# First stage of a two-layer diffusion backbone: the middle tokens' norm and scaling ordered ahead of the last tokens' squares, and the last tokens' norm issued inside the first projection

## Chip, cores, metric

The kernel runs on one core of a Trainium2 chip. The metric is the device time of one execution in microseconds (us), lower is better. The engines named below are TensorE (PE, matmuls into PSUM banks; PEld is its weight load), VectorE (DVE), ScalarE (ACT), GpSimd (POOL) and SyncE (SP, whose queue issues most of the DMAs). Each runs its own queue in order and waits for others through semaphores.

## What is computed

Two layers over 1024 latent tokens and 256 context tokens of width 1024. Cut to what matters for the change, the even layer begins with:

```python
def rms_norm(x, g):
    y = x * lax.rsqrt(jnp.mean(x * x, axis=-1, keepdims=True) + EPS)
    return y * g

sh, sc, g = jnp.split(silu(cond) @ mod_w + mod_b, 3, axis=-1)   # modulation; cond is c or c_ctx
h = rms_norm(x, norm_g) * (1.0 + sc) + sh                       # for latent and for context tokens
aq, ak, av, ag, bq, bk, bv, bg = split_cols(h @ w_in, EVEN_WIDTHS)   # queries, keys, values, gates
```

Behind it come two attentions (global, and banded with a sink), their gates, the output projection, the odd layer (a convolution module and neighbourhood attention) and a last norm.

## The kernel before

Activations are held transposed: 128 partitions by tokens, in DK = 8 row blocks `dk` of the width. The 1280 tokens are cut into three chunks (`CHUNKS`): chunk 0 is the context (256 tokens), chunk 1 the "middle" tokens (512), chunk 2 the "last" tokens (512). Every fp32 product is made as three matmuls: an operand is split into a rounded hi part and the rest, the lo part, and `mm3` runs hi by hi, hi by lo, and lo by hi (L334 to L336).

The first stage is a list of steps, `PLAN = 'p0mmnbwmm1h2nbhnbh'`, worked off in order (loop `for ev in PLAN`, L741). Digits load a chunk of x, `w` loads the first projection weights, and the others are:

- `m`: half a block of the modulation (`mod_half`): 8 matmuls `pm` with an output of 32 partitions (L184; 16 records in the profile), a copy `mrow` on ACT, 4 small matmuls `trm` (L189), and adds into `modT` and `gs`.
- `n`: `norm_x`: for each of 8 row blocks a square on ACT (L727 for the first, into `acc`, L730 for the others, into `sq`), and 7 dependent adds `acc += sq` on DVE (L731). `sq` has three buffers.
- `b`: `norm_bc`, which runs `rstd_steps`: matmuls `trs` (L261) sum `acc` over the partitions; DVE makes mean plus EPS in `rbv` (L264); `newton_rsqrt` takes a power on POOL (L246) and three small DVE steps (L247 to L249); matmuls `bc` (L271) spread the result over 128 partitions.
- `h`: `make_h`: for each row block a scaling on DVE (L324), a shift on ACT (L327, or L330 and a rounding in `split`, L314) that gives the hi part, and the lo part on DVE (L328) or POOL (L317), by the letters of `HV = 'gggvvvvg'`. The hi and lo parts are `hc` for chunk 0, `hh` and `hl` for the others.

The first projection follows: `fill0(0, w0)` runs `proj_qkv` and `proj_gate` for head group `ORDER[0]`. `proj_qkv` takes ten blocks `j` of 128 tokens (j = 0, 1 context, 2 to 5 middle, 6 to 9 last), each 8 x 3 matmuls `pq` of 384 columns with weights `wh`, `wl`; behind each pair come copies `pc` on ACT, V, the rotary steps, and later a transpose `trk` (L881) in `qk_tail`. `proj_gate` makes `pg`. Between the row blocks `tick()` advances `mods`, which loads and multiplies the rest of the modulation (again `pm`, `trm`).

The code gives each instruction its dependences and a priority; a scheduler places it in its engine's queue by its own estimate of when it can run, so code order and queue order differ. What is written under `tc.issue_after(ins)` is scheduled no earlier than `ins`. After the first projection, attention steps are woven with the other head groups' projections (`weave`), and the second layer follows.

Of the kernel before, what the change touches and what calls it, by code (L numbers as in the profile page):

```python
# [10 lines left out]
F32 = mybir.dt.float32  # L11
F32R = mybir.dt.float32r
ALU = mybir.AluOpType
# [59 lines left out]
TICK0, TICK1 = (1, 3)  # L73
PLAN = 'p0mmnbwmm1h2nbhnbh'
MWR = "ABxAVx"
XA = 4
ORDER = (2, 3, 0, 1)
QORD = (2, 3, 4, 0, 5, 6, 1, 7, 8, 9)
# [10 lines left out]
def tile_kernel(ctx: ExitStack, tc: tile.TileContext, a, out):  # L89
# [161 lines left out]

    last = []

    def rstd_steps(pool, accs, n, tag, inv=1.0, tr="tr"):


        nb = n // P
        tr = bank(tr, nm("trs"))
        for b in range(nb):
            for k, acc in enumerate(accs):  # L260
                last.append(PE.matmul(tr[:, 2 * b : 2 * b + 2], acc[:, b * P : (b + 1) * P], ones, start=(k == 0),  # L261
                                      stop=(k == len(accs) - 1)))
        v = pool.tile([P, 8], F32, tag="rbv", name=nm("rbv"), bufs=2)
        VE.tensor_scalar(v[:, :nb], tr[:, 0 : 2 * nb].rearrange("p (b two) -> p b two", two=2)[:, :, 0],  # L264
                         inv, EPS, op0=ALU.mult, op1=ALU.add)
        r = newton_rsqrt(pool, v[:, :nb], nb, "rb")
        yield
        yield
        bc = bank(tag, nm("bc"))
        for b in range(nb):  # L270
            PE.matmul(bc[:, b * P : (b + 1) * P], r[:, b : b + 1].broadcast_to([P, P]), ident, start=True, stop=True)  # L271
        return bc
# [45 lines left out]

    def make_h(l, c, xs, bc, h):

        cond = 1 if c == 0 else 0
        for dk in range(DK):
            x = xs(dk)
            VE.scalar_tensor_tensor(x, x, gs[l][:, dk, cond : cond + 1], bc, op0=ALU.mult, op1=ALU.mult)  # L324
            shift = modT[l][:, dk, cond : cond + 1]
            if HV[dk] == "v":
                SC.activation(h[0][:, dk, :], x, AF.Identity, bias=shift)  # L327
                VE.scalar_tensor_tensor(h[1][:, dk, :], x, shift, h[0][:, dk, :].bitcast(F32), op0=ALU.add, op1=ALU.subtract)  # L328
# [366 lines left out]
    with ExitStack() as p0x:  # L695
# [6 lines left out]
        with tc.tile_pool(name="st0", bufs=1, reuse_waits="tile") as st0:  # L702
# [19 lines left out]
            def norm_x(c):  # L722
                n = CHUNKS[c][1]
                acc = kvp.tile([P, 512], F32, tag="QH", name=nm("acc"), bufs=3)
                for dk in range(DK):
                    if dk == 0:
                        SC.activation(acc[:, :n], xraw[c][0], AF.Square)  # L727
                    else:
                        sq = kvp.tile([P, 512], F32, tag="QL", name=nm("sq"), bufs=3)
                        SC.activation(sq[:, :n], xraw[c][dk], AF.Square)  # L730
                        VE.tensor_tensor(acc[:, :n], acc[:, :n], sq[:, :n], op=ALU.add)  # L731
                return acc
# [5 lines left out]
            made = [0]  # L738
            accs, bcs, mh = [], [], [(0, 0), (0, 1), (1, 0), (1, 1)]
            mwp[0] = st0  # L740
            for ev in PLAN:  # L741
# [90 lines left out]
        def proj_qkv(u, w):  # L832
            wh, wl = w or load_w0("ev_qkv", u)
            new_kv(u)
            for jp in range(5):
                pc = ap.tile([P, 2, 384], F32, tag="pc", name=nm("pc"), bufs=PCB)
                for jj in range(2):
                    j = 2 * jp + jj
                    pp = bank("pp", nm("pq"))
                    for dk in range(DK):  # L840
                        mm3(pp[:, :384], Hs(h, 0, j * P, P, dk), Hs(h, 1, j * P, P, dk), wh[dk], wl[dk],
                            dk == 0, dk == DK - 1)
                        if dk % 3 == 1:
# [56 lines left out]

        for _ in fill0(0, w0):
            pass
        solo[0] = False
# [725 lines left out]
```

## Time and profile before

| | us |
|---|---|
| median of 3 runs (1553.38 to 1559.51) | 1554.67 |
| the profiled execution's own time | 1557.54 |
| its span in the profile | 1555.8 |
| TensorE busy in the span | 1462.5 |
| TensorE busy in the first 40 us | 26.06 |
| TensorE busy from 40 to 60 us | 13.25 |
| TensorE busy from 200 to 400 us | 194.27 |
| mean granted TensorE clock (1 is full) | 0.959 |

A row of the timeline reads: start, duration, engine, source line, operation, output tile <- input tiles, shape, count of merged instructions, and in brackets the idle time just before on that engine and what ended it. A row of the windows view reads: the stretch and its length, then for PE, PEld, DVE, ACT and POOL the busy time and the count of instructions, then the granted TensorE clock, the DMA share and GB/s. A sum that starts at one row and ends at another is worked out from starts, since neighbouring matmuls overlap in the rows.

### The profile page before, as it was taken

What the parts mean: (1) busy time and instruction counts of PE and PEld (TensorE: products, weight loads), DVE (VectorE), ACT (ScalarE), POOL (GpSimd) and SP (SyncE); (2) the same over time, 40 slices, a digit from 0 to 9 for tenths busy, and PEclk for the clock granted to TensorE, in tenths of its full rate; (3) what the DMA queues carried; (4) which work ended last, traced back from release to release, by engine and by line L of the source; (5) the groups of instructions that cost most, each with busy time, mean ns of one, the idle gap of its engine ahead of it and who ended that gap; (6) DMA issues with size and microseconds to landing.
All of it is one profiled execution on the core that took longest, in us unless ns stands there. A gap on an engine that the chain in (4) does not pass through costs nothing.

```text
span 1555.8 us, 21467 instructions
## 1 busy us (share of the span) xinstructions
PE 1462.5 (94%) x7084; PEld 1177.6 (76%) x7084; DVE 1046.0 (67%) x2113; ACT 747.6 (48%) x1418; POOL 800.2 (51%) x637
## 2 busy tenths in 40 slices
PE   6899999998998999999999889999999799989995
PEld 2776888896896778886877568888887688878874
DVE  2832466579678855567677848999756566577766
ACT  3721434444434564447656565443434455455562
POOL 3430334446455766557646665665632334364674
PEclk7899999999999999999999799999999899999996
DMA  9474315423312245121202021211446777877632
GB/s 365 150 247 136 102 61 174 149 65 98 114 55 77 86 145 196 45 79 43 58 28 80 23 65 60 60 48 41 152 158 212 208 220 234 257 231 230 191 86 108
DMA packets 154168, 199.83 MB, mean 128 GB/s; under 512 B 14716, under 2 KB 95816, under 8 KB 154056
## 3 DMA queue, kind: packets, MB, share of 16 engines
q1 hardware_dynamic: 147392, 186.88, 38.0%
q10 hardware_dynamic: 6664, 11.57, 2.2%
q8 instruction: 56, 0.92, 0.3%
q14 instruction: 56, 0.46, 0.1%
HBM read 148.07 MB, written 49.02 MB: 127 GB/s over the span
## 4 chain that ended last, share of the span: by engine, by line
PE 81%; DVE 11%; DMA 3%; issue 2%; ACT 2%; POOL 1%; SPq 0%; DVEq 0%; POOLq 0%; ACTq 0%
PE p L334 7%; PE p L336 7%; PE p L335 7%; PE ov L462 5%; PE ov L464 5%; PE ov L463 4%; PE st L511 4%; PE st L515 4%; PE po L334 4%; PE po L335 4%; PE po L336 4%; PE pq L334 3%; PE pq L335 3%; PE pq L336 3%; PE pg L334 2%
## 5 line engine op out<-in xcount | busy, mean ns | idle before, releaser
L317 POOL TENSOR_TENSOR pl<-pf,ph 128x512 fp32r<-128x512 f32 (+4 forms) x321 | 395.6, 1243 | 381.8 <-ACT ph L314 332.8
L523 ACT ACTIVATE pf<-st 128x512 f32<-128x512 f32 x284 | 166.2, 596 | 214.0 <-PE st L515 175.6
L317 POOL TENSOR_TENSOR wl<-wr,wh 128x512 fp32r<-128x512 f32 (+2 forms) x131 | 170.4, 1312 | 138.6 <-ACT wh L314 123.7
L314 ACT CAST ph<-pf 128x512 fp32r<-128x512 f32 (+4 forms) x364 | 209.3, 588 | 28.4 <-PE ov L463 16.3
L334 PE MATMUL p<-hh,wh 128*128 128x512 f32 x448 | 176.7, 395 | 3.0 <-DVE spv L317 1.4
L335 PE MATMUL p<-hl,wh 128*128 128x512 f32 x448 | 174.3, 390 | 0.0
L336 PE MATMUL p<-hh,wl 128*128 128x512 f32 x448 | 172.3, 390 | 0.0
L511 PE MATMUL st<-QH,KAt 128*128 128x512 f32 (+4 forms) x364 | 142.0, 391 | 7.5 <-ACT pf L523 6.7
L462 PE MATMUL ov<-ph,Vt 128*128 128x512 f32 (+4 forms) x364 | 143.3, 394 | 3.1 <-DVE y L672 2.0
L464 PE MATMUL ov<-pl,Vt 128*128 128x512 f32 (+4 forms) x364 | 142.4, 391 | 2.1 <-POOL pl L317 2.0
L463 PE MATMUL ov<-ph,Vt 128*64 128x512 f32 (+4 forms) x364 | 141.0, 387 | 0.0
L515 PE MATMUL st<-QL,KBt 68*128 68x512 f32 (+4 forms) x364 | 137.3, 388 | 2.0 <-DVE QL L440 1.9
L1099 DVE SCALAR_TENSOR_TENSOR cps<-U,taps,cps 128x512 f32<-128x512 f32 x184 | 126.0, 752 | 0.7
L314 ACT CAST wh<-wr 128x512 fp32r<-128x512 f32 (+2 forms) x134 | 81.0, 613 | 91.4 <-DMA wr<-in_od_d_dram 18.4
L334 PEld LDWEIGHTS p<-hh,wh 128*128 128x128 f32 x448 | 84.2, 188 | 21.8 <-ACT wh L314 1.9
L635 DVE TENSOR_REDUCE mp<-mx 128x1 f32<-128x512 f32 x128 | 85.3, 682 | 19.4 <-PE mx L634 18.5
L336 PEld LDWEIGHTS p<-hh,wl 128*128 128x128 f32 x448 | 84.2, 188 | 17.5
L335 PEld LDWEIGHTS p<-hl,wh 128*128 128x128 f32 x448 | 84.2, 188 | 16.8 <-issue 0.5
L334 PE MATMUL pq<-wh,hh 128*128 128x384 f32 x256 | 88.0, 344 | 2.8 <-ACT hh L314 2.8
L511 PEld LDWEIGHTS st<-QH,KAt 128*128 128x128 f32 x364 | 70.1, 193 | 24.9 <-ACT pf L523 9.9
L464 PEld LDWEIGHTS ov<-pl,Vt 128*128 128x128 f32 x364 | 71.0, 195 | 23.3 <-POOL pl L317 5.0
L956 DVE SCALAR_TENSOR_TENSOR x<-po,modT,x 128x512 f32<-128x512 f32 (+1 forms) x72 | 47.0, 658 | 61.0 <-PE po L336 60.5
(280 smaller groups left out, 3491.9 us busy)
## 6 DMA issues: line engine op xcount, KB each, us to landing
mw<-in_mod_w_dram SPq DMA_DIRECT2D x16, 1024.0 KB, 5.4
Q<-qs SPq DMA_DIRECT2D x40, 256.0 KB, 2.1
QH<-Q SPq DMA_DIRECT2D x80, 128.0 KB, 2.7
mw<-in_mod_w_dram SPq DMA_DIRECT2D x16, 512.0 KB, 6.9
wr<-in_od_d_dram SPq DMA_DIRECT2D x32, 256.0 KB, 3.1
wr<-in_ev_qkv_dram SPq DMA_DIRECT2D x16, 384.0 KB, 5.2
KAt<-KD SPq DMA_DIRECT2D x16, 384.0 KB, 5.9
wr<-in_od_wo_dram SPq DMA_DIRECT2D x22, 256.0 KB, 3.2
```

What stands on the lines that cost most here:

```text
L314: acts.append(SC.copy(hi, src))
L317: (GP if leng == "g" else VE).tensor_tensor(lo, src, hi.bitcast(F32), op=ALU.subtract)
L334: PE.matmul(o, lh, rh, start=first, stop=False)
L335: PE.matmul(o, lh, rl, start=False, stop=False)
L336: last.append(PE.matmul(o, ll, rh, start=False, stop=end))
L462: PE.matmul(o, V[:, 64:192], ph[:, :n], start=(t == 0), stop=False)
L463: PE.matmul(g.ov[0:64, q0 : q0 + n], V[:, 0:64], ph[:, :n], start=False, stop=False)
L464: PE.matmul(o, V[:, 64:192], pl[:, :n], start=False, stop=(last and g.sink is None))
L511: sts.append(PE.matmul(st[:, :n], KA[:, cs], g.QH[:, q0 : q0 + n], start=True, stop=False))
L515: PE.matmul(st[:, :n], KB[0:68, cs], g.QL[0:68, q0 : q0 + n], start=False, stop=True)
L523: acts.append(SC.activation(pf[:, :n], st[:, :n], AF.Exp, scale=1.0 if g.bias else SCALE))
L1099: VE.scalar_tensor_tensor(pc, uc, w, pc, op0=ALU.mult, op1=ALU.add)
```

## The change

The end of `PLAN` becomes `1nh2bh` in place of `1h2nbhnbh`: the three steps of chunk 2 leave it, and the squares of chunk 1 are asked for ahead of the context's `h` and of chunk 2's load; the second half (dk 4 to 7) of the context's scalings must stand behind the last add of chunk 1. Chunk 2's norm moves into the first projection, as three steps of a new function `start0` that runs `fill0(0, w0)`: behind its step 6 the squares and adds, behind step 13 the sums, power and Newton steps (the sums behind the projection matmul last issued), behind step 15 the spread and `make_h`. Chunk 2's squares stand behind the last rounding of the context, its adds from the second one on behind the last scaling of chunk 1, and the context's matmuls from j = 1, dk = 5 on behind the spread of chunk 1's norm. Its norm's small tiles take the names `ss` and `sr` in another pool. Nothing else is computed.

```diff
-PLAN = 'p0mmnbwmm1h2nbhnbh'
+PLAN = 'p0mmnbwmm1nh2bh'
+S2 = (6, 13, 15)
+BC1 = (1, 5)
...
-    def rstd_steps(pool, accs, n, tag, inv=1.0, tr="tr"):
+    last, bcm = [], []
+
+    def rstd_steps(pool, accs, n, tag, inv=1.0, tr="tr", pin=None, vn=("rbv", 8, "rb")):
...
-                last.append(PE.matmul(tr[:, 2 * b : 2 * b + 2], acc[:, b * P : (b + 1) * P], ones, start=(k == 0),
-                                      stop=(k == len(accs) - 1)))
-        v = pool.tile([P, 8], F32, tag="rbv", name=nm("rbv"), bufs=2)
+                with ExitStack() as cx:
+                    if pin is not None:
+                        cx.enter_context(tc.issue_after(pin.ins))
+                    last.append(PE.matmul(tr[:, 2 * b : 2 * b + 2], acc[:, b * P : (b + 1) * P], ones, start=(k == 0),
+                                          stop=(k == len(accs) - 1)))
+        v = pool.tile([P, vn[1]], F32, tag=vn[0], name=nm("rbv"), bufs=2)
...
-            PE.matmul(bc[:, b * P : (b + 1) * P], r[:, b : b + 1].broadcast_to([P, P]), ident, start=True, stop=True)
+            bcm.append(PE.matmul(bc[:, b * P : (b + 1) * P], r[:, b : b + 1].broadcast_to([P, P]), ident, start=True,
+                                 stop=True))
...
-    def make_h(l, c, xs, bc, h):
+    def make_h(l, c, xs, bc, h, pin=()):
...
-            VE.scalar_tensor_tensor(x, x, gs[l][:, dk, cond : cond + 1], bc, op0=ALU.mult, op1=ALU.mult)
+            with ExitStack() as cx:
+                if pin and dk >= DK // 2:
+                    cx.enter_context(tc.issue_after(pin[-1].ins))
+                xg = VE.scalar_tensor_tensor(x, x, gs[l][:, dk, cond : cond + 1], bc, op0=ALU.mult, op1=ALU.mult)
...
+        return xg
...
                 for dk in range(DK):
-                    if dk == 0:
-                        SC.activation(acc[:, :n], xraw[c][0], AF.Square)
-                    else:
-                        sq = kvp.tile([P, 512], F32, tag="QL", name=nm("sq"), bufs=3)
-                        SC.activation(sq[:, :n], xraw[c][dk], AF.Square)
-                        VE.tensor_tensor(acc[:, :n], acc[:, :n], sq[:, :n], op=ALU.add)
+                    with ExitStack() as cx:
+                        if c == 2:
+                            cx.enter_context(tc.issue_after(acts0[-1].ins))
+                        if dk == 0:
+                            SC.activation(acc[:, :n], xraw[c][0], AF.Square)
+                        else:
+                            sq = kvp.tile([P, 512], F32, tag="QL", name=nm("sq"), bufs=3)
+                            SC.activation(sq[:, :n], xraw[c][dk], AF.Square)
+                    if dk > 0:
+                        with ExitStack() as cx:
+                            if c == 2 and dk > 1 and sums:
+                                cx.enter_context(tc.issue_after(sums[-1].ins))
+                            add = VE.tensor_tensor(acc[:, :n], acc[:, :n], sq[:, :n], op=ALU.add)
+                if c == 1:
+                    sums.append(add)
...
-                    make_h(0, made[0], lambda dk, c=made[0]: xraw[c][dk], bcs[made[0]], h[made[0]])
+                    xg = make_h(0, made[0], lambda dk, c=made[0]: xraw[c][dk], bcs[made[0]], h[made[0]],
+                                sums if made[0] == 0 else ())
+                    if made[0] == 0:
+                        acts0.append(acts[-1])
+                    if made[0] == 1:
+                        sums.append(xg)
...
+                            if u == ORDER[0] and (j, dk) == BC1:
+                                cx.enter_context(tc.issue_after(bcm[-1].ins))
...
-        for _ in fill0(0, w0):
-            pass
+        def start0(w):
+            for k, _ in enumerate(fill0(0, w)):
+                if k == S2[0]:
+                    acc = norm_x(2)
+                if k == S2[1]:
+                    b2 = rstd_steps(ap, [acc], 512, "st", pin=last[-1], vn=("ss", 16, "sr"))
+                    next(b2)
+                if k == S2[2]:
+                    with tc.issue_after(last[-1].ins):
+                        bc = run(b2)
+                    make_h(0, 2, lambda dk: xraw[2][dk], bc, h[2])
+
+        start0(w0)
```

Three places show how the queues move. The changed kernel's line numbers are some 6 to 27 higher. In these rows the number behind a name tells tiles of one kind apart.

First place, TensorE between the context's last matmuls and the middle tokens' first. `pq_558` and `pq_588` (before) and `pq_489` and `pq_519` (now) are the context's two blocks; `trs_414` and `bc_427` belong to the middle tokens, `trs_483` to the last. Before:

```order
L336 MATMUL pq_558<-wh_287,hc_171 128x384
L336 MATMUL pq_588<-wh_287,hc_171 128x384
L261 MATMUL trs_414<-ones,acc_391 128x2 x4
L261 MATMUL trs_483<-ones,acc_460 128x2 x4
L271 MATMUL bc_427<-ident,nr_421 128x128 x4
L334 MATMUL pq_629<-wh_269,hh_172 128x384
```

Now, the place of the sums and, 15 rows further on, that of the spread, which 9 more context matmuls follow:

```order
L345 MATMUL pq_519<-wl_276,hc_171 128x384
L346 MATMUL pq_519<-wh_275,hc_171 128x384
L266 MATMUL trs_414<-ones,acc_347 128x2 x4
L344 MATMUL pq_489<-wh_281,hc_171 128x384
L345 MATMUL pq_489<-wl_282,hc_171 128x384
```

```order
L345 MATMUL pq_489<-wl_288,hc_171 128x384
L346 MATMUL pq_489<-wh_287,hc_171 128x384
L276 MATMUL bc_427<-ident,nr_421 128x128 x4
L344 MATMUL pq_519<-wh_281,hc_171 128x384
L345 MATMUL pq_519<-wl_282,hc_171 128x384
```

The middle tokens' sums moved ahead of the context's second half, their spread ahead of its last 9 matmuls, and the last tokens' sums left this place.

Second place, VectorE ahead of these sums. `acc_391` (before) and `acc_347` (now) are the middle tokens' squares, `xr_178` the context. Before:

```order
L731 TENSOR_TENSOR acc_391<-acc_391,sq_402 128x512
L324 SCALAR_TENSOR_TENSOR xr_178<-xr_178,gs_104,bc_265 128x256 x4
L731 TENSOR_TENSOR acc_391<-acc_391,sq_405 128x512
L328 SCALAR_TENSOR_TENSOR hc_171<-xr_178,modT_102,hc_171 128x256 x2
L731 TENSOR_TENSOR acc_391<-acc_391,sq_408 128x512
L328 SCALAR_TENSOR_TENSOR hc_171<-xr_178,modT_102,hc_171 128x256
L731 TENSOR_TENSOR acc_460<-acc_460,sq_462 128x512
L731 TENSOR_TENSOR acc_391<-acc_391,sq_411 128x512
```

Now:

```order
L748 TENSOR_TENSOR acc_347<-acc_347,sq_358 128x512
L748 TENSOR_TENSOR acc_347<-acc_347,sq_361 128x512
L748 TENSOR_TENSOR acc_347<-acc_347,sq_364 128x512
L748 TENSOR_TENSOR acc_347<-acc_347,sq_367 128x512
L333 SCALAR_TENSOR_TENSOR xr_178<-xr_178,gs_104,bc_265 128x256 x4
L337 SCALAR_TENSOR_TENSOR hc_171<-xr_178,modT_102,hc_171 128x256
L269 TENSOR_SCALAR rbv_419<-trs_414 128x4
```

The four last adds of the middle tokens stand together, and the context's second four scalings behind them.

Third place, TensorE at the end of the middle tokens' blocks. `bc_730` is the last tokens' spread, `pq_713` the last middle block, `pq_800` to `pq_937` the last tokens' four blocks, `pm_535` and `pm_669` the modulation's first two half-blocks of this stretch. Now:

```order
L276 MATMUL bc_730<-ident,nr_687 128x128
L186 MATMUL pm_535<-mw_498,csil 32x512 x4
L276 MATMUL bc_730<-ident,nr_687 128x128 x3
L346 MATMUL pq_713<-wh_287,hl_173 128x384
L344 MATMUL pq_713<-wh_287,hh_172 128x384
L345 MATMUL pq_713<-wl_288,hh_172 128x384
L346 MATMUL pq_713<-wh_287,hl_173 128x384
L908 MATMUL trk_782<-ident,pc_488 128x128 x3
L191 MATMUL trm_567<-msel,mrow_544 128x2 x4
L344 MATMUL pq_800<-wh_269,hh_174 128x384
L345 MATMUL pq_800<-wl_270,hh_174 128x384
L344 MATMUL pq_836<-wh_269,hh_174 128x384
```

Before, the spread stood 85 rows ahead of the first of these blocks, and the second half-block, `pm_715`, was scattered between a transpose and the second of them:

```order
L881 MATMUL trk_826<-ident,pc_628 128x128 x2
L184 MATMUL pm_715<-mw_642,csil 32x512
L881 MATMUL trk_826<-ident,pc_628 128x128
L184 MATMUL pm_715<-mw_642,csil 32x512 x3
L184 MATMUL pm_715<-mw_644,csil 32x512 x2
L334 MATMUL pq_836<-wh_269,hh_174 128x384
L184 MATMUL pm_715<-mw_644,csil 32x512
L335 MATMUL pq_836<-wl_270,hh_174 128x384
L184 MATMUL pm_715<-mw_644,csil 32x512
```

Now `pm_669` stands as two rows of four behind the first matmuls of the last tokens, and these four blocks begin side by side. Further on, the queues of TensorE, VectorE and ScalarE differ again where the first layer's attention ends (near 800 to 920 us of the profile before), by the order of the same instructions.

More of the change, by code (lines that the diff above doesn't have):

```diff
@@ L738, in tile_kernel @@
             made = [0]
-            accs, bcs, mh = [], [], [(0, 0), (0, 1), (1, 0), (1, 1)]
+            sums, acts0, accs, bcs, mh = [], [], [], [], [(0, 0), (0, 1), (1, 0), (1, 1)]
             mwp[0] = st0
@@ L840, in proj_qkv @@
                     for dk in range(DK):
-                        mm3(pp[:, :384], Hs(h, 0, j * P, P, dk), Hs(h, 1, j * P, P, dk), wh[dk], wl[dk],
-                            dk == 0, dk == DK - 1)
+                        with ExitStack() as cx:
+                            if u == ORDER[0] and (j, dk) == BC1:
+                                cx.enter_context(tc.issue_after(bcm[-1].ins))
+                            mm3(pp[:, :384], Hs(h, 0, j * P, P, dk), Hs(h, 1, j * P, P, dk), wh[dk], wl[dk],
+                                dk == 0, dk == DK - 1)
                         if dk % 3 == 1:
```

3 lines of the change are left out of this document (1 added, 2 removed).

## The prediction

> **What bounds the kernel now.** I began with the whole page: how busy each engine is, and the chain of work that ended last, followed back from the end.
>
> ```profile
> PE 1462.5 (94%) x7084; PEld 1177.6 (76%) x7084; DVE 1046.0 (67%) x2113; ACT 747.6 (48%) x1418; POOL 800.2 (51%) x637
> PE 81%; DVE 11%; DMA 3%; issue 2%; ACT 2%; POOL 1%; SPq 0%; DVEq 0%; POOLq 0%; ACTq 0%
> ```
>
> TensorE is the bound, so a change to the first stage is worth what it takes from TensorE's idle time there, less what it adds. Next I asked for busy time by stretch. The first number behind each stretch is its length, the next TensorE's busy time; PEclk is the granted clock.
>
> ```profile
> 49.20:52.50 3.30, 0.00 (x0) 0.01 (x1) 3.23 (x10) 1.15 (x2) 1.52 (x1) 0.99 0.14 27
> 56.40:59.00 2.60, 0.00 (x0) 0.00 (x0) 2.60 (x5) 1.90 (x4) 0.00 (x0) 0.50 0.00 0
> 59.00:133.00 74.00, 73.96 (x382) 54.81 (x383) 33.34 (x55) 29.60 (x64) 33.22 (x25) 0.98 0.59 199
> ```
>
> From 59 to 133 us TensorE is never idle (73.96 of 74.00). Ahead of it lie two stretches in which it does nothing. The timeline of TensorE tells what stands there: `trs` are the column sums of the squares, `bc` spreads the norm over the partitions, `pq` is the projection.
>
> ```profile
> 43.28 0.45 PE L334 MATMUL pq<-wh,hc 128*128 128x384 f32 x1 [0.25 <-ACT hc L327]
> 48.20 0.95 PE L261 MATMUL trs<-ones,acc 128*128 128x2 f32 x8
> 52.52 1.84 PE L261 MATMUL trs<-ones,acc 128*128 128x2 f32 x8 [3.38 <-DVE nt L248]
> 54.22 2.05 PE L271 MATMUL bc<-ident,nr 128*128 128x128 f32 x8
> 59.04 0.69 PE L334 MATMUL pq<-wh,hh 128*128 128x384 f32 x1 [2.76 <-ACT hh L314]
> ```
>
> The context's matmuls end at about 48.2, and the middle tokens' first one starts at 59.04. Between them TensorE runs the middle tokens' sums, waits, runs the last tokens' sums (which stand ahead of the middle tokens' spread in its queue), and only then spreads the middle tokens' norm. The timeline of VectorE says why the sums themselves are late:
>
> ```profile
> 38.83 2.29 DVE L731 TENSOR_TENSOR acc<-acc,sq 128x512 f32<-128x512 f32 x3 [1.18 <-ACT sq L730]
> 41.31 0.68 DVE L731 TENSOR_TENSOR acc<-acc,sq 128x512 f32<-128x512 f32 x1
> 41.91 1.65 DVE L324 SCALAR_TENSOR_TENSOR xr<-xr,gs,bc 128x256 f32<-128x256 f32 x4
> 46.37 3.48 DVE L731 TENSOR_TENSOR acc<-acc,sq 128x512 f32<-128x512 f32 x5
> 51.55 0.16 DVE L247 TENSOR_TENSOR nt<-nr,rbv 128x4 f32<-128x4 f32 x1
> 52.48 0.16 DVE L249 SCALAR_TENSOR_TENSOR nr<-nt,nr 128x4 f32<-128x4 f32 x1
> 56.31 5.36 DVE L324 SCALAR_TENSOR_TENSOR xr<-xr,gs,bc 128x512 f32<-128x512 f32 x8 [0.27 <-PE bc L271]
> ```
>
> The middle tokens' seven adds are mixed with the context's scalings (41.91) and the last tokens' adds (in the group at 46.37), and the Newton steps on the norm, 51.55 to 52.6, with more of these.
>
> **The change part by part.** *The middle tokens' norm.* Three dependent adds take 2.29, so one follows the next by (2.29 - 0.68) / 2 = 0.80. The fourth still ends at 41.99, since nothing ahead of it moves; the seventh ends at 41.99 + 3 x 0.80 = 44.4 and the sums can start there, against 48.20: 3.8 us earlier. The four context scalings now queue behind that add: 44.3 instead of 41.91, so the context's second half, 24 matmuls that began at 43.28, starts at about 45.5. This is a new wait for TensorE, at a place where it had to wait anyway. The scalings end at 45.95, the lo part behind them at 46.4, and then the mean of squares goes to the power on POOL:
>
> ```profile
> 50.00 1.52 POOL L246 TENSOR_TENSOR nr<-rbv,mhalf 128x4 f32<-128x4 f32 x1 [3.83 <-DVE rbv L264]
> ```
>
> The power took 1.52 here; the three Newton steps are 0.16 each, some 0.6 with the hand-overs where nothing stands between them. So the norm is ready at about 46.5 + 1.5 + 0.6 = 48.7. In TensorE's queue 15 context matmuls stand between the sums and the spread. Their spacing depends on the granted clock, by these two pairs of neighbours:
>
> ```profile
> 60.90 0.52 PE L334 MATMUL pq<-wh,hh 128*128 128x384 f32 x1
> 61.22 0.52 PE L335 MATMUL pq<-wl,hh 128*128 128x384 f32 x1
> ...
> 73.56 0.33 PE L336 MATMUL pq<-wh,hl 128*128 128x384 f32 x1
> 73.73 0.33 PE L334 MATMUL pq<-wh,hh 128*128 128x384 f32 x1
> ```
>
> It is 0.32 at half clock and 0.17 at full. At full clock the norm decides: spread at 48.7, 1.05 long, scalings at 49.75. At half clock the queue decides: sums 44.4 to 46.3, 15 x 0.32 = 4.8, spread from 51.1 for up to 2.05, less where the clock rises on the way: scalings at 52.7. Before, they started at 56.31; the first matmul came 59.04 - 56.31 = 2.73 later, and the order on ScalarE ahead of it (two shifts and a rounding) stays. So the middle tokens' projection starts **6.6 to 3.6 us** earlier. I take the middle, **-5.1**, since both clocks appear between 43 and 63 us before.
>
> *The last tokens' sums* (8 records, 0.95 at full clock) now stand inside the stretch without gaps: **+0.8**. Their squares and adds are hidden beside the projections: the last add should end about 12.6 after the scalings' start (eight scalings 5.36, four lo parts, seven adds), some 10 after the first middle matmul, and TensorE reaches the sums after 69 matmuls, 12 us. If that cover is gone, each us is paid.
>
> *The last tokens' spread.* Before, it ran at 63.62, and their scaled rows lay ready long before the first of them entered TensorE at 81.42 (both rows below). Now 25 matmuls, the spread and two others end the middle tokens' part, and the chain spread, scaling, shift, rounding has only this to hide behind: 4 matmuls (0.7), a transpose (0.33) and the modulation's transposes (0.8), together 1.85. These rows of TensorE and ScalarE give the chain's pieces:
>
> ```profile
> 63.62 1.05 PE L271 MATMUL bc<-ident,nr 128*128 128x128 f32 x8
> ...
> 58.38 0.60 ACT L314 CAST hh<-xr 128x512 fp32r<-128x512 f32 x1
> 66.86 0.28 ACT L862 CAST Vt<-pc 128x128 fp32r<-128x128 f32 x1
> 75.65 0.48 ACT L846 COPY pc<-pq 128x384 f32<-128x384 f32 x1
> 76.02 0.38 ACT L314 CAST qs<-trk 128x256 fp32r<-128x256 f32 x1
> ...
> 81.42 0.42 PE L334 MATMUL pq<-wh,hh 128*128 128x384 f32 x1
> ```
>
> ScalarE's queue there holds: copy of the last middle result (ready 0.85 after the spread, 0.4), shift of row block 0 (0.65), rounding for the queries (0.3), V (0.2), shift of row block 1 (0.65), rounding of row block 0 (0.6): 3.6 after the spread. TensorE waits 3.6 - 1.85 = **+1.8**; bounds 0 (if VectorE and ScalarE keep ahead) and 3.6 (if nothing hides it). While it waits, the queue behind it is the whole rest of the first projection.
>
> *The clock after that wait.* Nothing before shows it at this place. The nearest rows are two short waits later on, and the clock behind them:
>
> ```profile
> 881.57 0.57 PE L634 MATMUL mx<-KAt,QH 128*128 128x512 f32 x1 [1.12 <-DVE mp L635]
> 886.92 0.79 PE L634 MATMUL mx<-KAt,QH 128*128 128x512 f32 x1 [1.30 <-DVE mp L635]
> ...
> 883.00:885.00 2.00, 1.85 (x5) 1.16 (x4) 2.00 (x3) 1.97 (x5) 2.00 (x2) 0.50 0.00 0
> ```
>
> A wait of 1.12 was followed by half clock. From 59.04 the slow pace lasted 3.5 us, 11 matmuls at 0.32 instead of 0.17: 1.6. Bounds 0 and +1.6; I take **+1.0**. [...]
>
> *The modulation's matmuls.* They write 32 partitions each, and the profile shows that one alone takes as long as a group:
>
> ```profile
> 86.88 1.04 PE L184 MATMUL pm<-mw,csil 128*32 128x512 f32 x2
> 88.12 1.90 PE L184 MATMUL pm<-mw,csil 128*32 128x512 f32 x10
> 90.33 1.05 PE L184 MATMUL pm<-mw,csil 128*32 128x512 f32 x2
> 91.68 1.04 PE L184 MATMUL pm<-mw,csil 128*32 128x512 f32 x2
> 106.53 1.93 PE L184 MATMUL pm<-mw,csil 128*32 128x512 f32 x16
> ```
>
> The second half-block was scattered: the four rows sum to 5.0, or 4.75 with the overlap of about 0.07 at each start taken off; the third stood together, 1.85 for 16 on the same count. The new order puts the second together (-2.9) and splits the third by a transpose into 3, 1 and 4 matmuls, two records each (like the first two rows above, one turn more: +1.0): **-1.9**, bounds -2.9 and 0.
>
> *What else moves.* SP's queue asks for the modulation weights ahead of two gate blocks; these land more than 10 us before the gate, which follows four row blocks of projection. The power and the lo parts on POOL change places, with slack. Near 800 to 920 us the scheduler swaps some attention steps; by idle time alone nothing tells the sign, so 0, with bounds of -3 and +3.
>
> The sum: -5.1 + 0.8 + 1.8 + 1.0 - 1.9 = **-3.4**. The profiled execution took 1557.54 (span 1555.8 and 1.7 around it) and would take 1554.1; it lies 2.9 above the median of 1554.67, and on the median's scale the forecast is **1551.3**. Since TensorE is full behind 59 and the chain later is mostly TensorE, a start 3.4 earlier should reach the end.
>
> **Rivals.** *The whole gain stays.* If the last tokens' chain is hidden and the first start is at full clock: -6.6 + 0.8 - 1.9 = -7.7, with a little from the later order about -8.5: 1546. For it: VectorE and ScalarE have room (33.34 and 29.60 busy of 74). Against it: the chain is a queue, not a lack of room.
>
> *Everything is given back.* The start is at the late bound (-3.6), the return wait is 3.6 and the clock falls (+1.6): with +0.8 and -1.9 that is +0.5: 1555.
>
> *Slower through the later order.* Near 873 the eight scalings of layer 1 now stand ahead of the `QL` rows that the next scores need; before, they stood behind:
>
> ```profile
> 871.72 0.68 DVE L440 TENSOR_TENSOR QL<-trn,k_bd 4x512 fp32r<-4x512 f32 x1 [1.51 <-PE trn L439]
> ...
> 873.34 5.36 DVE L324 SCALAR_TENSOR_TENSOR x<-x,gs,bc 128x512 f32<-128x512 f32 x8 [0.21 <-PE bc L271]
> ...
> 883.42 2.85 DVE L328 SCALAR_TENSOR_TENSOR hl<-x,modT,hh 128x512 fp32r<-128x512 f32 x2
> ```
>
> TensorE has 22 matmuls of about 0.23, 5.1 us, between the spread and the scores that read `QL`, against 5.36 + 0.68 = 6.0. That costs 1, hence my bound of 3. But the next block's row maxima queue there too, and if that cover is spent early they pay the 5.36 in full, then another 5 for the four lo parts mixed between them (2.85 for two), at half clock another 2: +12 - 3.4 = about +8.6, 1563. It decides once the uncovered part exceeds 3.4.
>
> **How the numbers follow.** My forecast, a gain below 0.5%, has 0.60; the whole gain 0.20; all given back 0.12; slower through the later order 0.08. Half a per cent, 7.8 us, is about what a measurement of this kernel can tell from no change. So faster 0.20, same 0.72, slower 0.08. For the range I take the forecast with the bounds of the unknown terms and of the later order: 1545 (near the whole gain) to 1557 (all given back, and 2 for the later order).
>
> **What would show it.** In the changed profile: the middle tokens' sums on TensorE at about 44.4 to 45; their spread between 48.5 and 51, and the first middle projection between 52.4 and 55.5. No wait ahead of the last tokens' sums. A wait of 1 to 3 us on ScalarE's rounding ahead of the first matmul of the last tokens, at about 77 to 79, with the clock at half behind it. The second modulation half-block as one group of 16 in 1.9. The gate's first matmul, `pg` (row below), at 104 to 106 instead of 108.38. The prediction is wrong if that one comes before 102 or after 108, or if the shift seen there isn't the shift at the end, which would put the rest on the order near 800 to 920.
>
> ```profile
> 108.38 0.39 PE L334 MATMUL pg<-hc,gh 128*128 128x256 f32 x1
> ```

## The result and the profile after

| | before | changed |
|---|---|---|
| median of 22 runs each, us | 1556.46 (1551.00 to 1563.46) | 1551.82 (1546.74 to 1556.63) |
| ratio | 1 | 0.997, 95% interval 0.996 to 0.998 |
| profiled execution, us | 1557.54 (span 1555.8) | 1553.03 (span 1551.1) |
| mean granted clock | 0.959 | 0.967 |

The changed kernel is 0.3% faster, 4.6 us of 1556, where 3.4 were forecast. The page of the changed kernel, with the engines and the chain by engine:

```profile
PE 1455.7 (94%) x7084; PEld 1173.2 (76%) x7084; DVE 1046.6 (67%) x2113; ACT 749.4 (48%) x1418; POOL 802.5 (52%) x637
PE 79%; DVE 11%; DMA 4%; issue 2%; ACT 2%; POOL 1%; SPq 0%; DVEq 0%; POOLq 0%; ACTq 0%
```

The same 7084 matmul records take 6.8 us less busy time. As the shares hardly move, the places must be looked at. The windows of the first stage, in the stretches shown of before:

```profile
49.20:52.50 3.30, 3.30 (x17) 3.30 (x16) 0.68 (x4) 0.63 (x1) 0.00 (x0) 0.62 0.51 164
56.40:59.00 2.60, 2.56 (x12) 1.96 (x12) 2.60 (x4) 2.60 (x6) 2.60 (x2) 1.00 0.00 0
59.00:133.00 74.00, 71.78 (x385) 54.26 (x385) 36.76 (x59) 28.74 (x62) 31.21 (x24) 0.98 0.59 199
```

The two idle stretches are full now, and the full one has 2.2 us of idle time. TensorE's timeline tells both:

```profile
44.43 1.42 PE L266 MATMUL trs<-ones,acc 128*128 128x2 f32 x8 [1.78 <-DVE acc L748]
50.65 1.57 PE L276 MATMUL bc<-ident,nr 128*128 128x128 f32 x8
54.98 0.44 PE L344 MATMUL pq<-wh,hh 128*128 128x384 f32 x1 [1.19 <-ACT hh L320]
...
56.36 0.45 PE L346 MATMUL pq<-wh,hl 128*128 128x384 f32 x1 [0.40 <-POOL hl L323]
59.42 0.44 PE L346 MATMUL pq<-wh,hl 128*128 128x384 f32 x1 [0.47 <-POOL hl L323]
69.15 0.95 PE L266 MATMUL trs<-ones,acc 128*128 128x2 f32 x8
75.59 0.38 PE L276 MATMUL bc<-ident,nr 128*128 128x128 f32 x2
...
76.89 0.93 PE L276 MATMUL bc<-ident,nr 128*128 128x128 f32 x6
81.31 0.44 PE L344 MATMUL pq<-wh,hh 128*128 128x384 f32 x1 [1.66 <-ACT hh L320]
86.54 1.92 PE L186 MATMUL pm<-mw,csil 128*32 128x512 f32 x16
103.37 1.06 PE L186 MATMUL pm<-mw,csil 128*32 128x512 f32 x6
104.84 1.90 PE L186 MATMUL pm<-mw,csil 128*32 128x512 f32 x10
106.67 0.39 PE L344 MATMUL pg<-hc,gh 128*128 128x256 f32 x1
```

The sums start at 44.43, the middle tokens' projection at 54.98 (59.04 before), the last tokens' sums wait for nothing, and their first matmul waits 1.66. The gate comes at 106.67: only 1.7 of the 4.1 us are left there. Yet the span is 4.7 shorter, so the gate isn't the whole of it.

**How the runs are compared.** The first loads shift a whole execution by up to 2.4 us: the middle tokens' first square starts between 35.23 (the second profile of middle_only, below) and 37.65 (before). The middle tokens' first square on ScalarE, in the changed kernel and in the first experiment:

```profile
37.54 0.63 ACT L740 ACTIVATE acc<-xr 128x512 f32<-128x512 f32 x1
```

```profile
35.68 0.63 ACT L740 ACTIVATE acc<-xr 128x512 f32<-128x512 f32 x1 [1.33 <-DMA xr<-in_xT_dram]
```

So the table counts the first two columns from this square (37.65 in the profile of before). The others are distances in one profile: from the gate to the third head group's gate near 360, from there to the fourth's near 511, and the **late stretch** from the output projection's first `po` near 835 to layer 1's first `p` near 943, around the place where the prediction named a changed order. "2", "3": the kernel's further profiles (experiments 4, 6, 7 and 10). A **block of half clock**, below, is a stretch of 3.41 us at a granted clock of 0.50 (as from 82.44 to 85.86 in the changed kernel); a longer stretch counts as several.

| kernel | first middle `pq` | gate `pg` | to 360 | to 511 | late stretch | ratio to before (95%) |
|---|---|---|---|---|---|---|
| before | 21.39 | 70.73 | 251.18 | 151.79 | 108.43 | |
| before, 2 | 21.06 | 71.60 | 249.68 | 151.81 | 108.89 | |
| changed | 17.44 | 69.13 | 249.29 | 151.75 | 104.84 | 0.997 (0.996 to 0.998) |
| changed, 2 | 17.42 | 69.10 | 249.29 | 151.78 | 106.45 | |
| changed, 3 | 17.04 | 68.75 | 250.87 | 155.63 | 105.31 | 0.9972 (0.9953 to 0.9992) |
| spread_early | 17.44 | 64.55 | 249.21 | 155.41 | 106.00 | 0.9914 (0.9887 to 0.994) |
| spread_early, 2 | 17.43 | 64.56 | 248.02 | 154.74 | 104.51 | 0.9938 (0.9916 to 0.9959) |
| adds_mixed | 17.95 | 68.92 | 250.72 | 155.50 | 109.03 | |
| adds_mixed, 2 | 17.83 | 69.49 | 249.21 | 153.49 | 109.33 | 1.0006 (0.9989 to 1.0022) |
| middle_only | 19.00 | 65.91 | 247.23 | 155.29 | 106.60 | 0.992 (0.9896 to 0.9945) |
| middle_only, 2 | 18.50 | 64.68 | 247.32 | 151.94 | 105.42 | 0.9917 (0.9891 to 0.9943) |
| both_early | 15.43 | 62.55 | 248.45 | 155.60 | 103.13 | 0.9929 (0.9912 to 0.9947) |
| mixed_other_late | 17.96 | 68.38 | 249.26 | 153.34 | 104.84 | 0.9946 (0.9927 to 0.9965) |
| sums_behind | 19.86 | 66.46 | 251.13 | 151.77 | 106.69 | 0.9953 (0.9934 to 0.9973) |

### The profile page after: what moved, and what is told of

It reads as the page before. It is cut to its first block, busy times and chain, and to the rows that moved or that the text cites. A ratio compares the mean times of both kernels' runs of the same rounds, so it can differ in the third digit from the quotient of the medians.

```text
span 1551.1 us, 21457 instructions
## 1 busy us (share of the span) xinstructions
PE 1455.7 (94%) x7084; PEld 1173.2 (76%) x7084; DVE 1046.6 (67%) x2113; ACT 749.4 (48%) x1418; POOL 802.5 (52%) x637
## 4 chain that ended last, share of the span: by engine, by line
PE 79%; DVE 11%; DMA 4%; issue 2%; ACT 2%; POOL 1%; SPq 0%; DVEq 0%; POOLq 0%; ACTq 0%
PE p L344 7%; PE p L346 7%; PE p L345 7%; PE ov L472 4%; PE ov L474 4%; PE ov L473 4%; PE po L344 4%; PE st L521 4%; PE po L345 4%; PE po L346 4%; PE st L525 4%; PE pq L344 3%; PE pq L346 3%; PE pq L345 3%; PE pg L344 2%
## 5 line engine op out<-in xcount | busy, mean ns | idle before, releaser
L346 PE MATMUL pq<-wh,hl 128*128 128x384 f32 x256 | 86.7, 341 | 1.0 <-POOL hl L323 0.9
```

The lines of the kernel that those rows point to most:

```text
L346: last.append(PE.matmul(o, ll, rh, start=False, stop=end))
```

## The experiments

**1. The last tokens' spread earlier (spread_early).**

```diff
-                            if u == ORDER[0] and (j, dk) == BC1:
+                            if u == ORDER[0] and (j, dk) in (BC1, (5, 2)):
```

> The changed kernel with one more fixed place: the projection matmuls of the last middle block from j = 5, dk = 2 on must stand behind the spread of the last tokens' norm, so the spread stands about 15 matmuls earlier in TensorE's queue (norm ready at 71.97, spread then at about 73.5 instead of 75.6 to 76.9). My theory (the wait of 1.66 us before the last tokens' first matmul, and the half clock behind it, are both caused by the late spread): the wait is gone or under 0.3, no stretch at half clock follows near 82 to 86, the gate's first pg comes at 103.3 to 104.0 instead of 106.67, and the end moves by -2.5 to -3.3. Rival A (the clock falls there by itself, not because of the wait): half clock stays, pg at about 105.0, end -1.6. Rival B (ScalarE's queue, not the spread's place, holds the rounding): the wait stays over 1, pg within 0.7 of 106.67, end unchanged.

TensorE around the spread, and no row with a wait behind it up to the last tokens' blocks:

```profile
70.82 0.55 PE L908 MATMUL trk<-ident,pc 128*128 128x128 f32 x3
71.20 1.06 PE L276 MATMUL bc<-ident,nr 128*128 128x128 f32 x8
72.89 1.06 PE L186 MATMUL pm<-mw,csil 128*32 128x512 f32 x8
```

The spread starts 35.52 behind the first square (the changed kernel's two parts 38.05 and 39.35). Wait and half clock are both gone. From the first middle matmul to the gate it takes 47.11 instead of 51.69: worked out from the starts of all rows between, -1.64 waits, -1.55 in the 192 projection matmuls, -0.97 in the modulation's matmuls (the third half-block is no longer split), the rest in small pieces. The theory holds, and more came than it said.

**2. The adds mixed again (adds_mixed).**

```diff
-                                sums if made[0] == 0 else ())
+                                ())
```

> The changed kernel without the rule that the context's second four scalings stand behind the middle tokens' last add: adds, scalings and lo parts are mixed again on VectorE, while the last tokens' norm stays in the projection. My theory (the order of the adds sets the middle tokens' sums, and the norm's chain of 4.3 us behind them sets the start): sums at 47 to 48 instead of 44.43, first middle projection at 56.0 to 57.0 instead of 54.98 (59.04 before the change). Rival A (what counts is that the last tokens' sums no longer stand ahead of the spread; the order of the adds is hidden): start at 54.7 to 55.3. Rival B (the order of the adds is everything): start at 58.5 to 59.5.

The middle tokens' sums and spread in this kernel:

```profile
45.99 1.02 PE L266 MATMUL trs<-ones,acc 128*128 128x2 f32 x8 [0.93 <-DVE acc L748]
48.96 2.08 PE L276 MATMUL bc<-ident,nr 128*128 128x128 f32 x8 [1.95 <-DVE nr L251]
```

The sums are late again, 10.14 behind the first square (changed 6.89, before 10.55), but the projection starts only 0.5 later than in the changed kernel. The sums came as my theory said, the start did not, and rival A is nearly right: the spread comes 2.97 behind the sums here, and 6.22 in the changed kernel, where 15 context matmuls at 0.32 stand between. The gate, at 68.92, is as early as in the changed kernel, but in this profile no half clock follows the wait of 1.66 before the last tokens; in the kernel's second profile, where it does, the gate is at 69.49, later by about what the start is. So adds that stand together are worth some 0.5 at the gate. The end was another matter: see 6 and 8.

**3. The middle tokens' part alone (middle_only).**

```diff
-PLAN = 'p0mmnbwmm1h2nbhnbh'
+PLAN = 'p0mmnbwmm1nh2bhnbh'
...
-            VE.scalar_tensor_tensor(x, x, gs[l][:, dk, cond : cond + 1], bc, op0=ALU.mult, op1=ALU.mult)
+            with ExitStack() as cx:
+                if pin and dk >= DK // 2:
+                    cx.enter_context(tc.issue_after(pin[-1].ins))
+                VE.scalar_tensor_tensor(x, x, gs[l][:, dk, cond : cond + 1], bc, op0=ALU.mult, op1=ALU.mult)
```

> The kernel before with the middle tokens' part of the change alone: their squares are asked for first and their last adds stand ahead of the context's second four scalings, but the last tokens' squares, sums and spread stay in the first stage. TensorE's queue then has the context's matmuls, the middle tokens' spread, the last tokens' sums, and the middle tokens' projection. My theory (the late last tokens cost what is given back later): the middle tokens start later than in the changed kernel, at 55.5 to 57.5, since the last tokens' seven adds stand ahead of the scalings on VectorE; but no wait and no half clock stand before the last tokens' blocks, their sums fill idle time, and the modulation's second half-block stands in two rows of four, so pg comes at 102.5 to 105.5, before the changed kernel's 106.67. Rival (the middle tokens can only be early if the last tokens' norm is out of the way): start at 58 to 59.5, pg at 106 to 108.5, no faster than before by more than 2 us.

```profile
51.74 1.05 PE L271 MATMUL bc<-ident,nr 128*128 128x128 f32 x8
52.63 0.95 PE L261 MATMUL trs<-ones,acc 128*128 128x2 f32 x8
55.56 0.44 PE L337 MATMUL pq<-wh,hh 128*128 128x384 f32 x1 [1.97 <-ACT hh L314]
```

These are its spread, the last tokens' sums in time that TensorE waits anyway, and the first projection. It starts 1.6 later than the changed kernel and reaches the gate 3.2 earlier: 46.91 from the one to the other. Here too the second half-block of the modulation stands in rows of four: 5.84 for all modulation matmuls instead of 8.60. Taking the last tokens' norm into the projection, with its spread where the changed kernel has it, cost more than it brought.

**4. The changed kernel again (after_again).** No edit.

> The changed kernel once more, to see which parts of its shift recur. My theory: first middle projection at 54.98, gate at 106.67, each within 0.3; the extra shift of -1.85 between 134 and 157 us against the kernel before, and of -1.05 between 500 and 945, come from where the granted clock happens to rise and fall, so either may differ by 1 or more in this run. Rival (they belong to the changed order of the queue): both recur within 0.4, as the rest does.

The absolute times came some 1.5 earlier than said, as the first square did; by the table's counts start and gate recur within 0.1, and the extra shift between gate and 160 recurs. The part from 511 to 943 was -4.3 instead of -1.0: that one varies by itself. Neither theory covers both.

**5. Both spreads earlier (both_early).** As 1, and `BC1 = (1, 4)` instead of `(1, 5)`.

> The kernel of the first experiment (last tokens' spread early) and, besides, the context's matmuls held back behind the middle tokens' spread from j = 1, dk = 4 on instead of dk = 5, so that 12 instead of 15 of them stand between the middle tokens' sums and their spread. Counted from the middle tokens' first square on ScalarE, since the first loads shift whole executions by up to 2 us. My theory (the queue at half clock, not the norm, holds the spread): first middle projection at 16.3 to 16.7 behind that square (17.44 in the changed kernel), gate's first pg at 63.3 to 63.9 (64.55 in the first experiment), ratio to before 0.989 to 0.993. Rival (the chain behind the spread or the matmuls moved behind it eat this up): 17.2 to 17.6 and 64.3 to 64.8, ratio as without it.

Start 15.43 and gate 62.55, better than said. Part of this is the clock: half clock on the context's matmuls lasts one block here (their spacing is 0.32 up to 46.65 and 0.17 behind it), and two in the changed kernel (6.83 from 44.90, and 6.83 from 42.19 in its third profile). The ratio is that of 1 within the intervals.

**6. Experiments 1 and 2 timed again (spread_early_more, adds_mixed_more).** No new edits.

> The kernel of the first experiment again, timed in five rounds beside the others. My theory: gate's first pg 64.4 to 64.8 behind the first square, as in its first run; ratio to before 0.990 to 0.994, below the changed kernel's 0.996 to 0.998. Rival (its first time was luck): ratio 0.995 to 0.999.

> The changed kernel without the rule on the context's scalings, timed. In its first run the gate's first pg stood 68.92 behind the first square (changed kernel 69.13), but the run lost 3.7 us between 360 and 511, where TensorE's queue holds the same order as the changed kernel's, in three stretches of half clock of 3.41 each. My theory (the rule is worth nothing, and which stretches fall to half clock is a matter of the single execution): ratio to before 0.994 to 0.999, as the changed kernel's, and other stretches at half clock in this profile. Rival (mixing the adds costs time): ratio 1.000 to 1.004, the three stretches recur.

The first recurs. The second has no gain at all, 1.0006, though its gate is within 0.8 of the changed kernel's: the rival's ratio. Two of its three blocks of half clock between 360 and 511 did not recur, yet that stretch still took 153.49, so they are not the whole cause. The table shows what recurs: its late stretch takes 109, as before the change. In their queues, VectorE and POOL stand row for row as in the kernel before from some 155 us to the end, and TensorE's and ScalarE's differ at four and three places; in the changed kernel all four differ between 800 and 945 us.

**7. The kernel before again (before_again).** No edit.

> The kernel before once more, for its clock. Its first profile had half clock from 52.41 to 62.65 and from 137.74 to 141.16, and the latter is where the changed kernel gained its 1.9 us behind the gate. [...]

Windows of both profiles of before, first the profile shown so far, then this one:

```profile
134.33:137.74 3.41, 2.57 (x18) 1.97 (x16) 2.66 (x8) 1.11 (x3) 0.00 (x0) 1.00 0.97 364
137.74:141.15 3.41, 3.41 (x16) 3.41 (x17) 1.70 (x6) 0.60 (x1) 0.00 (x0) 0.50 0.52 198
```

```profile
134.44:137.86 3.42, 2.58 (x18) 1.98 (x17) 2.67 (x8) 1.11 (x3) 0.00 (x0) 1.00 1.01 368
137.86:141.27 3.41, 3.41 (x30) 3.41 (x31) 2.11 (x9) 0.97 (x2) 0.00 (x0) 1.00 0.50 187
```

The same work and the same waits, TensorE busy for 2.57 and for 2.58 of the first 3.41, and this time no half clock: the distance from the gate to 360 is 1.5 shorter. So 1.5 of the 1.9 us that the changed kernel seemed to gain there belong to the single execution; its third profile has such a block and 250.87.

**8. The late order by itself (mixed_other_late).** Experiment 2 with `S2 = (6, 14, 17)` instead of `(6, 13, 15)`. From some 120 to some 1200 us, TensorE, VectorE, ScalarE and POOL then stand as in the changed kernel, row for row.

> The kernel with mixed adds, with the last tokens' sums and spread asked for one and two steps later (behind steps 14 and 17 instead of 13 and 15). Its first stage is that of the mixed adds up to the last tokens' spread; but near 800 to 945 us its queues stand in the changed kernel's order, while the mixed adds' queues stood in the order of the kernel before. New theory (the end's gain comes from the order near 835 to 945, not from the first stage): from the first po near 835 to the first p near 943 it takes 104.5 to 106.7 us as in the changed kernel, the kernel with mixed adds having taken 109.0 and 109.3. Rival (that stretch takes what it takes because of the first stage): 108.5 to 109.5. In the first stage the spread now stands three matmul groups ahead of the last tokens' first matmul: by the prediction's working the wait there grows from 1.66 to 2.5 to 3.6, and the gate's first pg stands 69.6 to 71.0 behind the first square (68.92). Ratio to before: 0.996 to 1.000 by the new theory, 1.001 to 1.004 by the rival.

The late stretch takes 104.84, and the ratio is 0.9946 where experiment 2 had 1.0006, with a gate only 0.5 to 1.1 earlier. The new theory holds, and the ratio came out lower than the 0.996 to 1.000 that it gave. One part was wrong: the wait before the last tokens stayed at 1.64, since ScalarE had the copy and V behind it by the time that the later spread ended. The windows of the late stretch, first of experiment 2's second profile, then of this one:

```profile
835.92:945.25 109.33, 97.25 (x395) 72.78 (x393) 71.86 (x127) 63.23 (x114) 66.09 (x52) 0.84 0.19 65
```

```profile
831.55:936.39 104.84, 92.37 (x395) 69.08 (x394) 70.01 (x126) 64.13 (x115) 66.63 (x52) 0.90 0.20 68
```

TensorE idles 12.1 and 12.5 us: the same. It is busy 4.9 us less for the same 395 records, at a higher clock. The four profiles with the order of before have 9 or 10 blocks of half clock there, those of the changed kernel 6, 7 and 5. One difference is seen at the first wait, in TensorE's timeline of the kernel before and of the changed kernel:

```profile
861.31 0.77 PE L511 MATMUL st<-QH,KAt 128*128 128x512 f32 x1 [3.13 <-ACT pf L523]
```

```profile
858.24 0.50 PE L521 MATMUL st<-QH,KAt 128*128 128x512 f32 x1 [1.74 <-ACT pf L533]
860.35 0.52 PE L644 MATMUL mx<-KAt,QH 128*128 128x512 f32 x1 [1.08 <-DVE mp L645]
```

One wait of 3.13 became two with work between them. Half clock follows in both, for three blocks from 861.37 before and for two from 860.68 now. Which waits save the other blocks isn't shown.

**9. Only the last tokens' sums moved (sums_behind).** The kernel before, with this in `rstd_steps` (`bcm` collects the spread's matmuls):

```diff
+                    if len(bcm) == 6:
+                        cx.enter_context(tc.issue_after(bcm[-1].ins))
```

> The kernel before with one edit: the last tokens' sums must stand behind the middle tokens' spread in TensorE's queue; adds, scalings and Newton steps stay mixed as they were. Theory (it was the place of the last tokens' sums, waiting for their adds, that held the spread): the spread starts when the norm is ready, some 15.0 behind the middle tokens' first square instead of 16.6, the first middle projection at 19.4 to 20.0 (21.39 and 21.06 in the two profiles of before), the gate's first pg at 69.0 to 70.1 (70.73 and 71.60). Rival (the norm, mixed with the last tokens' adds on VectorE, holds it): 21.0 to 21.4, gate unchanged. Near 800 to 945 its order is again another one, whose worth is not foretold.

```profile
47.96 0.95 PE L264 MATMUL trs<-ones,acc 128*128 128x2 f32 x8
51.77 1.16 PE L274 MATMUL bc<-ident,nr 128*128 128x128 f32 x8 [2.87 <-DVE nr L249]
52.77 1.45 PE L264 MATMUL trs<-ones,acc 128*128 128x2 f32 x8
55.69 0.69 PE L338 MATMUL pq<-wh,hh 128*128 128x384 f32 x1 [1.47 <-ACT hh L318]
```

The start is 19.86, as the theory said: the place of these sums was worth 1.2 to 1.5 by itself. The spread follows the norm at once, but came 15.94 behind the square where 15.0 was expected: half clock (3.41 us from 42.81) slowed the context's matmuls, so the sums stand at 12.13 (10.55 and 12.06 in the two profiles of before, the second with the same half clock). The gate is 2.5 earlier than said, for the most part since the modulation's matmuls came out grouped here too (5.84 instead of 8.60).

**10. The changed kernel and the middle part timed again (after_timed, middle_only_more).** No edits.

> The changed kernel in five rounds beside the others. New theory: the gate's first pg at 69.0 to 69.2 behind the first square, the stretch from po near 835 to p near 943 at 104.5 to 106.7, ratio to before 0.995 to 0.998. Rival (the mixed adds' ratio of 1.0006 was that of the chip it ran on): ratio 0.999 to 1.002.

> The kernel with the middle tokens' part alone, in five rounds. Its queues near 835 to 945 stand in the changed kernel's order. Theory: gate's first pg at 65.7 to 66.2 behind the first square, the late stretch at 104.5 to 106.7, ratio to before 0.991 to 0.995. Rival (its first ratio of 0.992 was luck): 0.995 to 0.998.

Ratios and late stretches recur. The changed kernel's gate was 0.25 earlier than said. Middle_only's gate was 1.0 earlier than said: 0.5 at the start, and the wait of 0.42 behind it, seen in its first profile, was gone. The changed kernel's third profile lost 3.9 us between 360 and 511, as others did. The rows there, first of its first profile, then of this one:

```profile
375.99:379.40 3.41, 2.40 (x10) 1.30 (x8) 3.34 (x7) 1.38 (x3) 3.41 (x3) 1.00 0.45 153
379.40:382.82 3.42, 2.24 (x12) 1.54 (x13) 3.26 (x8) 1.12 (x4) 1.32 (x2) 1.00 0.19 70
```

```profile
376.70:380.11 3.41, 1.80 (x10) 0.94 (x8) 3.28 (x8) 1.07 (x4) 3.41 (x3) 1.00 0.49 154
380.11:383.52 3.41, 3.06 (x11) 2.13 (x10) 2.99 (x7) 0.92 (x4) 0.44 (x1) 0.50 0.22 80
383.52:386.94 3.42, 3.42 (x9) 2.65 (x9) 2.84 (x9) 2.61 (x5) 1.75 (x2) 0.50 0.23 79
```

The same kernel, and a wait of 1.42 in the first and 1.43 in the other. In the first the clock stays at 1.00; in the other two blocks of half clock follow, from 380.11.

## Why the time was right and the sum was not

1551.3 was forecast, 1551.82 measured, and "a gain below 0.5%" is what came. That the two times lie so close is partly luck: before took 1556.46 by 22 runs, 1.8 more than the median of 3 that the forecast starts from, and -3.4 from there would be 1553.1. But the prediction had named what would prove it wrong: a shift at the gate that isn't the shift at the end. That happened: -1.7 and -4.7. By its own steps, from the first square to the gate in the two profiles first compared:

| term | forecast | measured |
|---|---|---|
| middle tokens' projection starts | -5.1 (-6.6 to -3.6) | -3.95 |
| last tokens' sums | +0.8 | +0.81 |
| wait before the last tokens | +1.8 | +1.66 |
| two short waits for lo parts on POOL | not seen | +0.87 |
| half clock and spacing of the 192 projection matmuls | +1.0 | +0.58 |
| modulation's matmuls | -1.9 | -1.94 (8.60 to 6.66) |
| spread, transposes | 0 | +0.37 |
| sum at the gate | -3.4 | -1.60 |
| late order | 0 (-3 to +3) | -3.1 (means of 2 and 3 profiles) |

The second profile of before has its gate 0.9 later, though its projection starts 0.3 earlier; by the means of 2 and 3 profiles the shift at the gate is -2.2.

- **The start** was mis-sized: the slow pace was on, so the queue and not the norm set the spread, and the start came near the late bound. Its reason was partly wrong, too. The adds that stand together moved the sums by 3.3 and the start by 0.5 (experiment 2). Taking the last tokens' sums from ahead of the spread gave 1.2 to 1.5 (9), and the rest, 1.9 between experiments 9 and 2, with the last tokens' norm out of the first stage: the middle tokens' norm is ready 2.8 earlier there. Of this, 0.9 is its last steps, from the mean to the norm, which take 1.85 instead of 2.77 with the last tokens' adds gone from between the Newton steps; the other 2.0 is the sums, and what part of it is the clock isn't shown. The middle tokens' spread, at half clock in experiment 2 (2.08 instead of 1.16), takes some of it back.
- **The wait, the sums and the modulation** were as worked out, to 0.15. Two waits of 0.40 and 0.47 on POOL were overlooked: with an early start two lo parts are needed before POOL has them.
- **The clock** fell behind the wait, a whole block:

```profile
79.03:82.44 3.41, 1.75 (x12) 1.67 (x12) 3.41 (x6) 3.41 (x9) 1.57 (x2) 1.00 0.71 267
82.44:85.86 3.42, 3.42 (x13) 3.42 (x12) 3.42 (x6) 3.42 (x7) 3.42 (x4) 0.50 0.22 78
```

It costs 1.6: in the two profiles of experiment 2, the 192 projection matmuls take 37.34 with such a block and 35.78 without. The term came out smaller since before paid such a block at 59.24, which the sum didn't take off; the 0.58 that is left is spacing that these rows don't explain. The block was in all three profiles of the changed kernel, but that was partly chance: it followed the same wait in one of the three profiles of experiments 2 and 8 (last section).

- **The step that failed** is the later reorder: "by idle time alone nothing tells the sign, so 0". Idle time was indeed the same, and so the wrong thing to ask. The late order lies at the bound, -3.1, by fewer blocks of half clock. The two errors largely cancelled: 1.8 too much in the first stage, 3.1 too little behind it. Of the rival with layer 1's scalings ahead of `QL` the order came, but not the cost: `QL` is made at 876.53 behind them, and the longest wait that follows on the row maxima is 2.31, where it was 1.30 before.

That the late order shortens the late stretch is shown by ten profiles. The four with the order of before, from two first stages, take 108.43 to 109.33; the six with the changed kernel's order, from three first stages (the changed kernel, experiments 3 and 8), take 104.84 to 106.60. In the changed kernel this is 3.1, by the means, of the 4.6. Experiments 2 and 8 share the first stage up to the last tokens' spread and differ by 0.6%, some 9 us; the late stretch has 4.3 of them and the gate 0.5 to 1.1. The rest between them isn't resolved: the stretch from 511 to 835 takes between 319 and 328 in all these profiles without a pattern, and the two also differ in order behind 1200. The kernel before's first stage with the late order of the changed one wasn't tried.

The faster versions keep the last tokens' norm in the first stage (3), or spread it earlier (1): 0.9914 to 0.9938, with intervals that overlap.

## What to carry to other kernels

Where a scheduler sets the order, a small edit can change the order far from its place and be worth more there: compare the whole queues, and time a version with the same edit and the other order. When a wait is removed, look at what stands between the two ends in the queue, since the next thing there may hold it as well. Before crediting an edit with the loss or return of a stretch of half clock, profile the same kernel twice.

## What the runs showed of the hardware

In the first profiles of the kernel before and of the changed kernel, each stretch of half clock lasts 3.41, 6.83, 10.24 or 13.65 us, except the one that runs to the end. Five starts in the changed kernel, 44.90, 82.44, 522.76, 744.63 and 1208.84, lie 11, 129, 65 and 136 times 3.413 us apart. Where they fall in the program differs by profile: the block behind the wait before the last tokens starts 44.90 behind the first square in this one (82.44 - 37.54) and 43.60 in the changed kernel's third (79.74 - 36.14).

How long TensorE was busy in the 3.41 us ahead didn't decide alone whether half clock followed. It followed 1.75 (from 79.03 in the changed kernel), 1.80 (from 376.70 in its third profile), 2.57 (from 134.33 in the kernel before) and even 3.36 (from 1516.73 there). It didn't follow 2.40 and 2.24 (from 375.99 and 379.40 in the changed kernel), 2.58 (from 134.44 in the second profile of before), nor 1.75 (from 472.51 in experiment 8).

Nor did the length of the wait alone: half clock followed the wait of 1.43 near 380 in the changed kernel's third profile and not that of 1.42 in its first (experiment 10). So it is with the wait of 1.64 to 1.66 before the last tokens, which six profiles have. In four, the changed kernel's three and the second of experiment 2, half clock follows; in the first of experiment 2 and in experiment 8 none does. What decides isn't shown. The wait and the windows of experiment 2's first profile:

```profile
80.08 0.44 PE L344 MATMUL pq<-wh,hh 128*128 128x384 f32 x1 [1.66 <-ACT hh L320]
```

```profile
76.09:79.50 3.41, 2.33 (x20) 2.21 (x18) 2.86 (x5) 2.52 (x7) 0.46 (x1) 1.00 0.96 332
79.50:82.92 3.42, 2.84 (x16) 2.84 (x17) 3.42 (x7) 3.42 (x8) 2.82 (x3) 1.00 0.34 127
```

Each block costs TensorE up to 1.7, an estimate: half of the 3.41 that it lasts, since the granted clock is 0.50. The one behind the wait of 1.66 cost 1.6.
